# A triangular inverse carried through DRAM in fewer transfers, with longer steps behind it and behind a group norm

## The chip, the cores and the metric

The kernel runs on one core of one Trainium2 chip. The metric is the device time of one execution in microseconds (us). Two numbers are used: the time of a run, of which the median of three is given, and the span of one profiled execution, from its first instruction to its last. The engines are named as in the profile: PE (TensorE, matrix products), PEld (its weight loads), DVE (VectorE), ACT (ScalarE), POOL (GpSimd) and SP (SyncE, which here issues almost every DMA).

## What is computed

One inference step of a one-layer encoder over 16 meta tokens, 256 prompt tokens and 64 sample tokens, with a model width of 2048. One input projection feeds two branches: a Mamba-2 scan (SSD, 32 heads in 4 groups) and a gated DeltaNet (16 heads, in 4 groups of 4 here). Their outputs go through one output projection and are merged by sigmoid gates; an MLP with squared ReLU and a final norm follow. The two places that the change touches are these:

```python
# SSD branch, once for each group
ya = _rmsnorm(ya.reshape(b, l, SSD_GROUPS, -1), ssd_norm_w.reshape(SSD_GROUPS, -1))

# DeltaNet branch, once for each block of 64 tokens and each head
lmat = jnp.where(strict, bc[..., :, None] * jnp.einsum('bhtk,bhsk->bhts', kc, kc) * decay, 0.0)
tinv = lax.linalg.triangular_solve(eye + lmat, jnp.broadcast_to(eye, lmat.shape),
                                   left_side=True, lower=True, unit_diagonal=True)
u = jnp.einsum('bhts,bhsv->bhtv', tinv, vc * bc[..., None])
```

## The kernel before

All matrix products with weights are done in three passes on split operands: a weight tile `raw` comes by DMA (512 KB, a slice of 512 rows by 256 columns), ACT copies its rounded part to `hi` (line 61, a helper), DVE subtracts to get `lo` (line 64, a helper), and PE runs 24 matmuls on a slice (8 places times three passes; `hi` with the high and the low part of the activations, `lo` with the high part), writing `pbig`. `raw`, `hi` and `lo` have three buffers each. A block is 4 slices of an input or gate projection, or 1 slice of an output projection.

**Main work and side work.** `run(main, side)` interleaves two generators. `main` is weight matmuls and yields the nominal microseconds of each three passes; `side` is a scan (`scan_ssd` or `scan_gdn`), which emits some instructions and then yields a number: so many nominal microseconds of main work are put ahead of its next instructions. That number is no wait on the chip; it only places instructions. What is left of `side` when `main` has ended is emitted at once. PE keeps exactly this order (`manual_schedule` for PE); the order on the other engines and of the DMAs on SP comes from a scheduler which orders by readiness. Every engine then runs its own list in order and waits on semaphores.

The runs that matter here are, in this order: `scan_ssd(0)` beside `proj_ssd(1)`; `scan_ssd(1)` and `scan_ssd(2)` each beside an output projection and the next input projection; `scan_ssd(3)` beside `out_a(2)` and `proj_gdn(0)`; then `scan_gdn(0)` beside `out_a(3)`, `gate_a` and `proj_gdn(1)`; `scan_gdn(1)` and `scan_gdn(2)` beside an output projection and the next DeltaNet projection; `scan_gdn(3)` beside `out_b(2)` and `gate_b`. Then come the last output projection and the MLP, with next to no side work.

**The SSD norm.** In `scan_ssd`, for each of three chunks `c`: ACT squares `yz` into `sq`, POOL adds its four parts in two instructions, then `yield 7.0` (line 718). `rstd_bcast` (line 594) sums over the partitions with a matmul into `prs`, DVE scales it (`r`, line 599), POOL takes the power -0.5, DVE spreads it over a diagonal (`dg`, line 602), then `yield 4.2`, and a matmul broadcasts it into `prb`. Four DVE instructions apply it to `yz`, ACT rounds that to `yh` and DVE takes the rest `yl`. After chunk 2 of group 0 the output projection `out_a(0)` reads `yh` and `yl` directly behind the run.

**The triangular inverse.** In `scan_gdn`, each of 12 matrices (3 chunks, 4 heads) of 128x128 is inverted by diagonal blocks of 32x32 first. The matrices `a` are stored to the DRAM scratch `aD`; `diag(ad, c)` (line 135) views the 16 diagonal blocks of one chunk, one block to a partition, and they are loaded into `ab`, twice (partitions 0 to 47 and 64 to 111, since each half of the partitions solves 16 of the 32 columns). The substitution (line 844) runs 31 steps on DVE, `s` from 30 down to 0: a product `pr` and a reduction into column `s` of `ubt` (line 851), each step yielding 0.5 + 0.0028 times its size. Step `s` writes column `s` alone, and columns 16 to 31 are final once `s` = 15 is done. When all steps are done:

- ACT copies `ubt`, transposed, into `ub` (line 856, two instructions of 48x512), and three DMAs store `ub` to the diagonal blocks of `uD` (line 858);
- two DMAs store `ubt` to `uTD` (line 861);
- three DMAs load the whole matrices from `uD` into `u` (line 863, one for each chunk);
- three DMAs load transposed blocks from `uTD` into `tr` (line 869).

Then `yield 9.6` (line 871), and PE joins the blocks: first `pz` from `tr` and `a` (32x32), then `ptr` and `pu` with `u`, then the same for 64x64. The copy `z` of `pz`, the three chunks' outer loop and the state update follow.

Of the kernel before, what the change touches and what calls it, by code (L numbers as in the profile page):

```python
# [8 lines left out]
F32 = mybir.dt.float32  # L9
# [5 lines left out]
P = 128  # L15
# [11 lines left out]
BS = 32  # L27
# [15 lines left out]
def tile_hybrid_step(ctx: ExitStack, tc: tile.TileContext, i: dict, o: dict):  # L43
    nc = tc.nc
# [15 lines left out]
    def act(out, in_, func=AF.Copy, **kw):  # L60
        nc.scalar.activation(out=out, in_=in_, func=func, **kw)  # L61

    def tt(eng, out, a, b, op):
        eng.tensor_tensor(out=out, in0=a, in1=b, op=op)  # L64
# [67 lines left out]
    def whole(t, c, n=P):  # L132
        return t[c, :, :P * P].rearrange("h (s t) -> s h t", t=P)[:n, :, :n]

    def diag(t, c):
        r = t[c].rearrange("h (b r) -> (h b) r", r=BS * P + BS)
        return r[:, :BS * P].rearrange("q (s t) -> q s t", t=P)[:, :, :BS]


# [454 lines left out]
    def rstd_bcast(pool, ssum, n, width):  # L594

        pc = scr("prs")
        mm(pc[:n, 256:257], ssum[:, :n], ones[:, 0:1])
        r = pool.tile([P, 1], F32, tag="r1", name="r1", bufs=2)
        V.tensor_scalar(out=r[:n], in0=pc[:n, 256:257], scalar1=1.0 / width, scalar2=EPS, op0=MUL, op1=ADD)
        tt(G, r[:n], r[:n], nhalf_pow[:n, 0:1], ALU.pow)  # L600
        dg = pool.tile([P, P], F32, tag="dg", name="dg", bufs=2)
        V.tensor_scalar(out=dg[:n, :n], in0=ident[:n, :n], scalar1=r[:n, 0:1], scalar2=None, op0=MUL)
        yield 4.2
        pr = scr("prb")
        mm(pr[:, :n], ones[:n, :], dg[:n, :n])
        return pr[:, :n]

    def scan_ssd(g, sg, x4, bc, z4):
# [25 lines left out]
        for c in range(3):  # L634
            lo, n, l0, nl, o0 = CH_LO[c], CH_N[c], L_LO[c], L_N[c], O_LO[c]
# [79 lines left out]
            act(sq[:, :, :nl], yz[:, :, :nl], AF.Square)  # L715
            tt(G, sq[:, 0:2, :nl], sq[:, 0:2, :nl], sq[:, 2:4, :nl], ADD)
            tt(G, sq[:, 0, :nl], sq[:, 0, :nl], sq[:, 1, :nl], ADD)
            yield 7.0
            rb = yield from rstd_bcast(sg, sq[:, 0, :], nx, 512)
            rb = rb[:, :nl]  # L720
            yh, yl = ys[g] = ys.get(g) or new_y()
# [15 lines left out]
    def scan_gdn(g, sg, q4, k4, v4, z4):  # L737
        heads = range(4)
        hsl = slice(32 + g * 4, 32 + g * 4 + 4)
        ad, ud = aD[g % 2], uD[g % 2]  # L740
        def t2k(tag, name, bufs):
            return sg.tile([P, 4, P], F32, tag=tag, name=name, bufs=bufs)
# [25 lines left out]
        for c in range(3):  # L768
            lo, n, l0, nl, o0 = CH_LO[c], CH_N[c], L_LO[c], L_N[c], O_LO[c]
# [54 lines left out]
        NB = 12 * (P // BS)  # L824
        nb, HB = NB // 3, BS // 2
        NE = 64 + NB
        ab = sg.tile([P, BS, BS], F32, tag="TZ", name="ab", bufs=1)
        G.memset(ab, 0.0)

        ubt = t2k("Ak", "ubt", 1).rearrange("p h (t s) -> p (h t) s", s=BS)  # L830
        uf = ubt.rearrange("p t s -> p (t s)")
        G.memset(uf, 0.0)
        for e in range(2):
            b = slice(e * 64, (e + 1) * 64)
            for c in range(3):
                nc.sync.dma_start(ab[e * 64 + c * nb:e * 64 + (c + 1) * nb], diag(ad, c))
            o1 = e * HB
            G.memset(uf[b, o1:o1 + (HB - 1) * (BS + 1)].rearrange("p (s t) -> p s t", t=BS + 1)[:, :, 0], 1.0)
            o1 += (HB - 1) * (BS + 1)
            G.memset(uf[b, o1:o1 + 1], 1.0)  # L840

        af = ab.rearrange("p s t -> p (s t)")[:NE, :HB * (BS + 1)]
        yield 4.8
        G.memset(af.rearrange("p (s t) -> p s t", t=BS + 1)[:, :, 0], 1.0)
        for s in range(BS - 2, -1, -1):
            j0, r0 = (s + 1 - HB, s + 1) if s >= HB else (0, s)
            w, m = HB - j0, BS - r0
            pr = t2k("sq", "pr", 2).rearrange("p h c -> p (h c)")
            v = pr[:NE, :w * m].rearrange("p (t r) -> p t r", r=m)
            tt(V, v, ubt[:NE, j0:, r0:], ab[:NE, s:s + 1, r0:].to_broadcast([NE, w, m]), MUL)  # L850
            V.tensor_reduce(out=ubt[:NE, j0:, s], in_=v, axis=AX.X, op=ADD)  # L851
            yield 0.5 + 0.0028 * w * m
        u = sg.tile([P, 3, 4, P], F32, tag="U", name="u")
        ub = sg.tile([P, BS, BS], F32, tag="XW", name="ub", bufs=1)
        for e in range(2):
            act(ub[:NB, :, e * HB:(e + 1) * HB].rearrange("p s t -> p t s"), ubt[e * 64:e * 64 + NB])
        for c in range(3):
            nc.sync.dma_start(diag(ud, c), ub[c * nb:(c + 1) * nb])
        utd = uTD[g % 2]
        for e in range(2):  # L860
            nc.sync.dma_start(utd.rearrange("c h b t s -> (c h b) t s")[:, e * HB:(e + 1) * HB], ubt[e * 64:e * 64 + NB])
        for c in range(3):
            nc.sync.dma_start(u[:, c], whole(ud, c))

        tr = sg.tile([P, 12, 64], F32, tag="TZ", name="tr", bufs=1)
        G.memset(tr[:BS, :8, BS:], 0.0)
# [1 line left out]
            b0, b1 = b * BS, (b + 1) * BS  # L868
            nc.sync.dma_start(tr[b0:b1, :, (b % 2) * BS:(b % 2 + 1) * BS], utd[:, :, b].rearrange("c h t s -> t (c h) s"))
        tr = tr.rearrange("p (c h) t -> p c h t", h=4)  # L870
        yield 9.6

        for r, pairs, cs in ((32, (0, 64), (0, 1, 2)), (64, (0,), (0, 1))):
            every = [(q, c, h) for c in cs for h in heads for q in pairs if q == 0 or c]
# [4 lines left out]
            for q, c, h in every:  # L879
                b, d = slice(q, q + r), slice(q + r, q + 2 * r)  # L880
# [14 lines left out]
            for q, c, h in every:  # L895
                b, d = slice(q, q + r), slice(q + r, q + 2 * r)
                mm(pu[b, c, h], z[d, c, h], u[d, c, h, d])
            for q in pairs:
                b, d, c0 = slice(q, q + r), slice(q + r, q + 2 * r), 1 if q else 0
                V.tensor_copy(u[b, c0:len(cs), :, d], pu[b, c0:len(cs)])  # L900
            yield 1.5
        for c in range(3):
            lo, n, l0, nl, o0 = CH_LO[c], CH_N[c], L_LO[c], L_N[c], O_LO[c]
# [150 lines left out]
    with ExitStack() as sctx:  # L1054
        sg = sctx.enter_context(tc.tile_pool(name="sg", bufs=1))
        run(kept(proj_ssd(1), tiles), scan_ssd(0, sg, *tiles[0]))
        run(chain(out_a(0), kept(proj_ssd(2), tiles)), scan_ssd(1, sg, *tiles[1]))
        run(chain(out_a(1), kept(proj_ssd(3), tiles)), scan_ssd(2, sg, *tiles[2]))
        run(chain(out_a(2), kept(proj_gdn(0), tiles)), scan_ssd(3, sg, *tiles[3]))
    with ExitStack() as sctx:  # L1060
        sg = sctx.enter_context(tc.tile_pool(name="sgg", bufs=1))
        run(chain(out_a(3), gate_a(), kept(proj_gdn(1), tiles)), scan_gdn(0, sg, *tiles[4]))
        run(chain(out_b(0), kept(proj_gdn(2), tiles)), scan_gdn(1, sg, *tiles[5]))
        run(chain(out_b(1), kept(proj_gdn(3), tiles)), scan_gdn(2, sg, *tiles[6]))
        run(chain(out_b(2), gate_b()), scan_gdn(3, sg, *tiles[7]))

        hnh, hnl = new_u("hn")
        h2 = const.tile([P, NO], F32, name="h2")

        def normed(k):  # L1070
            d, w = acc[:, k, :], par[:, NP_ + k:NP_ + k + 1]
            act(hnh[:, k, :NO], d, AF.Copy, scale=w)
            stt(hnl[:, k, :NO], d, w, hnh[:, k, :NO].bitcast(F32), MUL, SUB)

        def merge(k, pt):
            d, q = acc[:, k, :], ftile("q")
            tt(V, q, sgb[k // 4][:, k % 4, :], pt, MUL)
            tt(V, d, d, q, ADD)
            if k >= LAG:
                normed(k - LAG)  # L1080

        run(out_proj(3584, ys[7], False, merge))
        for k in range(KD - LAG, KD):
            normed(k)
# [117 lines left out]
    with tc.manual_schedule():  # L1202
        for t in range(3):
            final_part(7, t)
            r, n = frs[:, t:t + 1], toks[t][1]
            stt(r[n], fss[n, t, 7:8], 1.0 / D, fsum[n, t:t + 1], MUL, ADD)
            tt(G, r[n], r[n], nhalf_pow[n, 0:1], ALU.pow)
        for m in range(2):
            for t, (_, n, t0) in enumerate(toks):
                dst = o["y_prompt"][0, t0:t0 + P, :] if t < 2 else o["y_sample"][0]  # L1210
                w, r = slice(m * H, (m + 1) * H), frs[n, t:t + 1]
# [36 lines left out]
```

## Time and profile before

| | before |
|---|---|
| median of 3 runs | 2376.53 us |
| lowest and highest of them | 2375.6 and 2377.53 us |
| the profiled execution, its time | 2375.45 us |
| its span | 2373.7 us |
| mean granted TensorE clock | 0.989 |
| DVE busy, share of the span | 1356.8 us, 57% |
| ACT busy | 1060.3 us, 45% |
| POOL busy | 345.9 us, 15% |
| moved by DMA | 362.87 MB, mean 153 GB/s |

How to read the lines that follow below. A line of the waits names an engine, a line of the code, what it wrote, and what it waited for, with the total, the number of times and the longest. A line of the timeline has the start, the duration, the engine (SPq is the DMA issue on SP), the line, the operation, out<-in, and in brackets the idle time in front of it and what ended it. A line of the chain has start, duration, engine and name. A line of the windows has a stretch, its length, the busy time and count of PE, PEld, DVE, ACT and POOL, the granted TensorE clock (1.00 is full), the DMA engines' busy share and GB/s. Lines 58, 61, 64 and 67 are helpers, so the names of the tiles tell which work it is.

### The profile page before, as it was taken

How to read it: one execution, taken by the hardware profiler on the slowest of the kernel's cores; microseconds unless marked ns; L12 is line 12 of the kernel's file. 1: busy time of each engine (PE TensorE's matmuls, PEld its weight loads, DVE VectorE, ACT ScalarE, POOL GpSimd, SP SyncE). 2: the span in 40 equal slices, each digit the busy share in tenths (PEclk: the TensorE clock that was granted, in tenths of full speed). 3: DMA queues.
4: the chain of work that ended last, by engine and by line, in shares of the span. 5: the costliest groups of instructions: out<-in, count | busy, mean ns of one | idle time of the engine just before them, and what ended most of it. 6: DMA issues, size and time to landing. Idle time of an engine off the chain costs nothing.

```text
span 2373.7 us, 40688 instructions
## 1 busy us (share of the span) xinstructions
PE 2308.9 (97%) x16393; PEld 2284.7 (96%) x16393; DVE 1356.8 (57%) x2147; ACT 1060.3 (45%) x1822; POOL 345.9 (15%) x488
## 2 busy tenths in 40 slices
PE   7999999999999999899899999999999999999997
PEld 6999999999999999899899999999999999999997
DVE  6675858575855557568557558444444444444444
ACT  5655546355345544454454335433343234334433
POOL 3152515051211113112212110000000000000000
PEclk9999999999999999999899999999999999999999
DMA  7846555545556555454455544544554444445543
GB/s 194 222 123 182 143 158 154 156 131 172 158 166 185 150 152 144 127 154 134 127 152 149 158 144 149 148 151 151 151 151 150 146 150 151 150 151 151 169 142 115
DMA packets 411558, 362.87 MB, mean 153 GB/s; under 512 B 48841, under 2 KB 408346, under 8 KB 410906
## 3 DMA queue, kind: packets, MB, share of 16 engines
q1 hardware_dynamic: 411258, 360.15, 51.8%
q8 instruction: 128, 2.10, 0.4%
q14 instruction: 60, 0.49, 0.1%
q10 hardware_dynamic: 112, 0.13, 0.0%
HBM read 340.57 MB, written 19.66 MB: 152 GB/s over the span
## 4 chain that ended last, share of the span: by engine, by line
PE 85%; DVE 9%; DMA 2%; issue 1%; ACT 1%; POOL 1%; SPq 0%; ACTq 0%; DVEq 0%; POOLq 0%
PE pbig L58 78%; DVE lo L64 3%; DVE ubt L851 2%; DVE pr L64 1%; DVE c L67 1%; PE po L58 1%; DMA raw<-in_w_in_dram 1%; DMA tr<-uTD 1%; POOL yz L64 1%; PE pS L58 0%; PE pw L58 0%; ACT hi L61 0%; PE pkk L58 0%; PE pqk L58 0%; DVE ul L67 0%
## 5 line engine op out<-in xcount | busy, mean ns | idle before, releaser
L64 DVE TENSOR_TENSOR lo<-raw,hi 128x1024 fp32r<-128x1024 f32 x591 | 739.1, 1251 | 692.5 <-ACT hi L61 689.1
L61 ACT ACTIVATE hi<-raw 128x1024 fp32r<-128x1024 f32 x592 | 626.2, 1058 | 915.0 <-PE pbig L58 859.0
L58 PE MATMUL pbig<-uh,hi 128*128 128x320 f32 (+2 forms) x2176 | 692.5, 318 | 4.2 <-ACT uh L61 4.2
L58 PE MATMUL pbig<-uh,lo 128*128 128x320 f32 (+2 forms) x2176 | 683.9, 314 | 6.3 <-DVE lo L64 6.3
L58 PE MATMUL pbig<-ul,hi 128*128 128x320 f32 (+2 forms) x2176 | 685.0, 315 | 3.9 <-DVE ul L67 3.9
L58 PEld LDWEIGHTS pbig<-uh,hi 128*128 128x128 f32 x2176 | 413.5, 190 | 10.0 <-ACT uh L61 4.7
L58 PEld LDWEIGHTS pbig<-uh,lo 128*128 128x128 f32 x2176 | 413.4, 190 | 7.9 <-DVE lo L64 7.9
L58 PEld LDWEIGHTS pbig<-ul,hi 128*128 128x128 f32 x2176 | 413.5, 190 | 6.0 <-DVE ul L67 5.8
L58 PE MATMUL pbig<-hh,hi 128*128 128x320 f32 x1024 | 318.4, 311 | 0.0
L58 PE MATMUL pbig<-hnl,hi 128*128 128x320 f32 x1024 | 317.5, 310 | 0.0
L58 PE MATMUL pbig<-hl,hi 128*128 128x320 f32 x1024 | 316.7, 309 | 0.0
L58 PE MATMUL pbig<-hh,lo 128*128 128x320 f32 x1024 | 316.6, 309 | 0.0
L58 PE MATMUL pbig<-hnh,lo 128*128 128x320 f32 x1024 | 316.2, 309 | 0.0
L58 PE MATMUL pbig<-hnh,hi 128*128 128x320 f32 x1024 | 315.5, 308 | 0.0
L58 PEld LDWEIGHTS pbig<-hnh,lo 128*128 128x128 f32 x1024 | 193.2, 189 | 0.0
L58 PEld LDWEIGHTS pbig<-hl,hi 128*128 128x128 f32 x1024 | 193.0, 188 | 0.0
L58 PEld LDWEIGHTS pbig<-hh,hi 128*128 128x128 f32 x1024 | 193.0, 188 | 0.0
L58 PEld LDWEIGHTS pbig<-hh,lo 128*128 128x128 f32 x1024 | 192.9, 188 | 0.0
L58 PEld LDWEIGHTS pbig<-hnh,hi 128*128 128x128 f32 x1024 | 192.7, 188 | 0.2
L58 PEld LDWEIGHTS pbig<-hnl,hi 128*128 128x128 f32 x1024 | 192.4, 188 | 0.0
L58 PE MATMUL pbig<-yh,hi 128*128 128x320 f32 x512 | 161.4, 315 | 0.0
L58 PE MATMUL pbig<-yl,hi 128*128 128x320 f32 x512 | 157.7, 308 | 0.3 <-DVE yl L64 0.3
(303 smaller groups left out, 2436.8 us busy)
## 6 DMA issues: line engine op xcount, KB each, us to landing
raw<-in_w_in_dram SPq DMA_DIRECT2D x256, 512.0 KB, 3.8
raw<-in_w_up_dram SPq DMA_DIRECT2D x128, 512.0 KB, 3.8
raw<-in_w_down_dram SPq DMA_DIRECT2D x128, 512.0 KB, 3.4
raw<-in_w_out_dram SPq DMA_DIRECT2D x64, 512.0 KB, 3.5
raw<-in_w_in_dram SPq DMA_DIRECT2D x32, 256.0 KB, 3.5
em<-rowd SPq DMA_DIRECT2D x8, 512.0 KB, 7.7
u<-uD SPq DMA_DIRECT2D x12, 256.0 KB, 3.8
eab<-rowd SPq DMA_DIRECT2D x8, 336.0 KB, 8.5
```

The source lines that it names most:

```text
L58: nc.tensor.matmul(out, lhsT=lhsT, rhs=rhs, start=start, stop=stop, **kw)
L61: nc.scalar.activation(out=out, in_=in_, func=func, **kw)
L64: eng.tensor_tensor(out=out, in0=a, in1=b, op=op)
L67: nc.vector.scalar_tensor_tensor(out=out, in0=a, scalar=s, in1=b, op0=op0, op1=op1)
L851: V.tensor_reduce(out=ubt[:NE, j0:, s], in_=v, axis=AX.X, op=ADD)
```

## The change

Four edits; nothing else of the program text differs.

1. `diag` views all three chunks at once. So `ab` is loaded by two DMAs in place of six, `ub` is stored by one in place of three, and `u` is loaded by one in place of three. The bytes and the pieces that they consist of are the same.
2. `ub` is allocated ahead of the substitution, and its copy is cut by columns: columns 16 to 31 are copied (two ACT instructions of 48x16x16) at the head of step `s` = 14, the other half when the substitution is done.
3. The step behind the DMAs yields 15.0 in place of 9.6.
4. The step behind the sum of squares in `scan_ssd` yields 8.4 in place of 7.0.

```diff
-    def diag(t, c):
-        r = t[c].rearrange("h (b r) -> (h b) r", r=BS * P + BS)
+    def diag(t):
+        r = t.rearrange("c h (b r) -> (c h b) r", r=BS * P + BS)
...
-            yield 7.0
+            yield 8.4
             rb = yield from rstd_bcast(sg, sq[:, 0, :], nx, 512)
...
-            for c in range(3):
-                nc.sync.dma_start(ab[e * 64 + c * nb:e * 64 + (c + 1) * nb], diag(ad, c))
+            nc.sync.dma_start(ab[e * 64:e * 64 + NB], diag(ad))
...
+        def rows(s0):
+            for e in range(2):
+                act(ub[:NB, s0:s0 + HB, e * HB:(e + 1) * HB].rearrange("p s t -> p t s"), ubt[e * 64:e * 64 + NB, :, s0:s0 + HB])
+
         for s in range(BS - 2, -1, -1):
+            if s == HB - 2:
+                rows(HB)
...
-        for e in range(2):
-            act(ub[:NB, :, e * HB:(e + 1) * HB].rearrange("p s t -> p t s"), ubt[e * 64:e * 64 + NB])
-        for c in range(3):
-            nc.sync.dma_start(diag(ud, c), ub[c * nb:(c + 1) * nb])
+        rows(0)
+        nc.sync.dma_start(diag(ud), ub[:NB])
...
-        for c in range(3):
-            nc.sync.dma_start(u[:, c], whole(ud, c))
+        nc.sync.dma_start(u.rearrange("p c h t -> p (c h) t"), ud.rearrange("c h r -> (c h) r")[:, :P * P].rearrange("n (s t) -> s n t", t=P))
...
-        yield 9.6
+        yield 15.0
```

On PE the order changes only in place. Counted in the two programs, the first `pz` of DeltaNet groups 0, 1, 2 and 3 stands 39, 42, 42 and 39 weight matmuls later. In SSD group 0 the `prs` of chunk 1 stands 21 weight matmuls later, chunk 2's first `pyo` 21 later, chunk 2's `prs` 30 later and its `prb` 24 later, which is the end of that run's weight matmuls: `out_a(0)` follows directly, where 24 weight matmuls stood between before. In groups 1 to 3 the `prs` of the last chunk stands 30 to 33 later and 87 or more weight matmuls still follow `prb` in the run.

On SP, behind the substitution of DeltaNet group 1, the DMAs stood before as follows (`uTD`, `uD` the scratch in DRAM, `raw` a weight slice):

```order
L861 DMA uTD_112<-ubt 48x512 x2
L858 DMA uD_110<-ub 16x32x32 x3
L863 DMA u<-uD_110 128x4x128 x2
L869 DMA tr<-uTD_112 32x12x32
L863 DMA u<-uD_110 128x4x128
L869 DMA tr<-uTD_112 32x12x32 x2
L198 DMA raw<-in_w_in_dram 128x4x256 x5
```

In the changed program the same place reads:

```order
L865 DMA uTD_112<-ubt 48x512
L862 DMA uD_110<-ub 48x32x32
L865 DMA uTD_112<-ubt 48x512
L198 DMA raw<-in_w_in_dram 128x4x256
L866 DMA u<-uD_110 128x12x128
L872 DMA tr<-uTD_112 32x12x32 x3
L198 DMA raw<-in_w_in_dram 128x4x256 x7
```

All `tr` loads now stand behind the single `u` load, which waits for the whole store of `ub`, and one weight slice stands between. In groups 0 and 3 two `tr` loads stand ahead of `u` and one behind it.

On DVE, at the end of the first SSD run (`r`, `dg` and `yz` belong to chunk 2 of group 0; `em` is the decay tile of group 1's first chunk, which comes by DMA), the difference of the two programs is:

```order
-L599 TENSOR_SCALAR r_2119<-prs 128x1
-L602 TENSOR_SCALAR dg<-ident,r_2119 128x128
-L664 TENSOR_SCALAR em<-em,acs 128x128 x4
-L64 TENSOR_TENSOR lo<-raw,hi 128x1024
-L664 TENSOR_SCALAR em<-em,acs 128x128 x4
+L664 TENSOR_SCALAR em<-em,acs 128x128 x8
+L599 TENSOR_SCALAR r_2155<-prs 128x1
+L602 TENSOR_SCALAR dg<-ident,r_2155 128x128
+L64 TENSOR_TENSOR lo<-raw,hi 128x1024
 L67 SCALAR_TENSOR_TENSOR yz<-yz,par,prb 128x128 x4
 L64 TENSOR_TENSOR yl<-yz,yh 128x4x128
```

The eight instructions on `em` move from behind `dg` to ahead of `r`, so `r` and `dg`, and with them `prb`, come after the transfer that brings `em`.

On ACT, in DeltaNet group 0, the two rows `ub<-ubt 48x16x32 x2` stood together behind the substitution. Now two pairs of half the size stand there, one of them within it (`sgt` is the sigmoid of the gate):

```order
+L61 ACTIVATE ub<-ubt 48x16x16 x2
+L61 ACTIVATE hi<-raw 128x1024
+L61 ACT_TABLE_LOAD
+L61 ACTIVATE sgt<-pbig 128x320
+L61 ACTIVATE hi<-raw 128x1024
+L61 ACTIVATE sgt<-pbig 128x320
+L61 ACTIVATE hi<-raw 128x1024 x3
+L61 ACTIVATE sgt<-pbig 128x320
+L61 ACTIVATE hi<-raw 128x1024
+L61 ACTIVATE sgt<-pbig 128x320
+L61 ACTIVATE hi<-raw 128x1024 x2
+L61 ACTIVATE ub<-ubt 48x16x16 x2
```

The first pair moved ahead of the second by eight weight splits and four `sgt`. On DVE no instruction of the substitution waits for ACT in either program.

More of the change, by code (lines that the diff above doesn't have):

```diff
@@ L844, in scan_gdn @@
         G.memset(af.rearrange("p (s t) -> p s t", t=BS + 1)[:, :, 0], 1.0)
+        ub = sg.tile([P, BS, BS], F32, tag="XW", name="ub", bufs=1)
+        def rows(s0):
+            for e in range(2):
+                act(ub[:NB, s0:s0 + HB, e * HB:(e + 1) * HB].rearrange("p s t -> p t s"), ubt[e * 64:e * 64 + NB, :, s0:s0 + HB])
         for s in range(BS - 2, -1, -1):
+            if s == HB - 2:
+                rows(HB)
             j0, r0 = (s + 1 - HB, s + 1) if s >= HB else (0, s)
@@ L853, in scan_gdn @@
         u = sg.tile([P, 3, 4, P], F32, tag="U", name="u")
-        ub = sg.tile([P, BS, BS], F32, tag="XW", name="ub", bufs=1)
-        for e in range(2):
-            act(ub[:NB, :, e * HB:(e + 1) * HB].rearrange("p s t -> p t s"), ubt[e * 64:e * 64 + NB])
-        for c in range(3):
-            nc.sync.dma_start(diag(ud, c), ub[c * nb:(c + 1) * nb])
+        rows(0)
+        nc.sync.dma_start(diag(ud), ub[:NB])
         utd = uTD[g % 2]
```

## The prediction

> **What bounds the kernel now.** I read the page first, then PE's waits, then for each stretch in which PE waits the timelines, the chain and the windows.
>
> ```profile
> PE 2308.9 (97%) x16393; PEld 2284.7 (96%) x16393; DVE 1356.8 (57%) x2147; ACT 1060.3 (45%) x1822; POOL 345.9 (15%) x488
> PE pz L58 <- DMA tr<-uTD: 24.3, 8, 7.4
> PE prs L58 <- POOL sq L64: 3.7, 4, 1.6
> ```
>
> PE is busy for 97% of the span and its order is fixed, so the kernel is the sum of its matmuls and of what PE waits. The change adds no matmul and removes none; it can only change waits, and the speed at which PE works around them. The two waits that it aims at are the first and one of the next in the list: 24.3 us and 3.7 us. They are met four times each, once for each group (eight entries for `pz`, since it waits for two of the three `tr` loads).
>
> ```profile
> PE pz L58 <- DMA tr<-uTD: 4.5, 2, 3.4
> PE pz L58 <- DMA tr<-uTD: 8.1, 2, 7.4
> PE pz L58 <- DMA tr<-uTD: 7.6, 2, 7.1
> PE pz L58 <- DMA tr<-uTD: 4.0, 2, 3.3
> ```
>
> These are the same wait in groups 0, 1, 2 and 3 of the DeltaNet scan, each from the waits of a window around it.
>
> ```profile
> 674.30:677.70 3.40, 3.40 (x39) 3.34 (x40) 0.00 (x0) 0.86 (x2) 1.08 (x2) 0.50 0.95 290
> 969.90:974.60 4.70, 4.69 (x45) 4.29 (x46) 0.00 (x0) 0.86 (x2) 0.26 (x1) 0.50 0.49 163
> 1153.40:1162.40 9.00, 9.00 (x107) 8.54 (x108) 0.97 (x2) 1.23 (x3) 0.26 (x1) 0.50 0.26 86
> 1335.10:1339.90 4.80, 4.78 (x48) 4.39 (x49) 0.17 (x1) 1.92 (x3) 0.00 (x0) 0.50 1.07 352
> 970.97 3.54 PE pbig L58 x12
> 1036.04 27.64 PE pbig L58 x189
> ```
>
> The windows behind the four waits show a second cost that the list of waits hides. PE is busy all through them, but at a granted clock of 0.50: 3.4 + 4.7 + 9.0 + 4.8 = 21.9 us. The chain says what that means: there 12 weight matmuls took 3.54 us (0.295 each), where 189 undisturbed ones took 27.64 (0.146 each). So the work in these 21.9 us would take about 11.0 us less at full clock. The waits cost not 24.3 but some 35 us.
>
> **The DeltaNet part.** How long must the step be? Group 0, from the last reduction of the substitution to the arrival of `tr`:
>
> ```profile
> 662.47 0.69 DVE L851 TENSOR_REDUCE ubt<-pr 112x16 f32<-112x512 f32 x1
> 663.19 2.35 ACT L61 ACTIVATE ub<-ubt 48x512 f32<-48x512 f32 x2 [2.26 <-DVE ubt L851]
> 665.57 1.46 SPq L858 DMA_DIRECT2D uD<-ub  x3
> 667.87 0.93 SPq L863 DMA_DIRECT2D u<-uD  x2
> 670.45 3.71 DMA tr<-uTD
> 674.21 1.01 PE pz L58 x30
> 665.50:668.30 2.80, 2.80 (x21) 2.80 (x20) 1.64 (x3) 2.77 (x5) 0.00 (x0) 1.00 0.50 66
> ```
>
> The reduction ends at 663.16 and `pz` runs at 674.21: 11.0 us. PE stood ready 4.5 us earlier, at 669.7, which is 6.5 us after the reduction. The change puts 39 (groups 0, 3) or 42 (groups 1, 2) weight matmuls in between, at 0.146 us 5.7 or 6.1 us. So if the chain stays as long as it is, group 0 has 6.5 + 5.7 = 12.2 us for 11.0, and group 3, whose wait was 4.0, the like.
>
> Does the chain stay as long? The copy into `ub` on it halves: 1.2 us in place of 2.35. Of the three stores one is issued, 0.5 us in place of 1.46, but `u` must wait for all of it. The first of the three was there 2.3 us after its issue (665.57 to 667.87). A store three times as large is not in the trace. From below it lands as that one did, in 2.3; from above three follow each other, 6.9. The window of these stores decides which is nearer: the DMA engines were half busy for 2.8 us with all three in it, 1.4 us of work at most, so two thirds more of it, 0.9 us, comes on top of 2.3, and I take 3.2. Then one issue of `u` (0.47, half of the 0.93 for two), three of `tr` at the same rate, and 3.7 until the last lands, as now: 1.2 + 0.5 + 3.2 + 0.5 + 1.4 + 3.7 = 10.5 us. The fewer transfers thus give only 0.5 us; it is the longer step that takes the wait away.
>
> ```profile
> 956.91 0.68 DVE L851 TENSOR_REDUCE ubt<-pr 112x16 f32<-112x512 f32 x1
> 969.91 1.06 PE pz L58 x30
> 1141.64 0.69 DVE L851 TENSOR_REDUCE ubt<-pr 112x16 f32<-112x512 f32 x1
> 1153.38 1.05 PE pz L58 x30
> ```
>
> In groups 1 and 2 less time is left. The reductions end at 957.6 and 1142.3, `pz` runs at 969.9 and 1153.4, and without its wait it would have stood at 961.8 and 1145.8, 4.2 and 3.5 us after the reduction. With 6.1 more that is 10.3 and 9.6 us for a chain of 10.5, plus 0.5 for the issue of the weight slice that the new order puts ahead of `u`. So 0.7 and 1.4 us of wait are left. Against that, the new order has the last reduction two weight splits earlier on DVE in these groups, which may take it away; I keep 1.0 for both together. The term is **-23.3 us** (from -24.3 to -10).
>
> The clock follows the wait. A wait of 1.5 us left it at 1.00 (the row of 164.00 below), one of 3.4 us and more did not. With no wait over 1.5 us the 11.0 us go. The small matmuls of 32x32 in these windows may not scale with the clock; were it the weight matmuls alone, the loss by the chain's rows of this kind is near 8 us. I take the middle, **-9.5 us** (from -11 to -3). [...]
>
> The early copy into `ub` stands on ACT, which is busy for 45% of the span; its 1.2 us are hidden by that idle time. If the cover were gone, a weight split would come 1.2 us later, four times. The merged loads of `ab` start behind the last store of `a`, where three of the six stood before; the substitution hides them.
>
> **The SSD part.** In groups 1 to 3 the longer step removes the wait of `prs`: 3.7 less the 1.5 of group 0 is **-2.2 us**, and the 1.4 nominal us cost nothing, since 87 and more weight matmuls still follow. Group 0 is different:
>
> ```profile
> PE prs L58 <- POOL sq L64: 1.5, 1, 1.5
> 164.00:165.00 1.00, 0.07 (x1) 0.07 (x1) 0.00 (x0) 0.99 (x2) 0.80 (x2) 1.00 0.00 0
> 192.59 0.29 DVE L602 TENSOR_SCALAR dg<-ident,r 128x128 f32<-128x128 f32 x1 [0.67 <-POOL r L64]
> 196.26 0.88 DVE L664 TENSOR_SCALAR em<-em,acs 128x128 f32<-128x128 f32 x4 [3.38 <-DMA em<-rowd]
> 198.97 1.12 DVE L67 SCALAR_TENSOR_TENSOR yz<-yz,par,prb 128x128 f32<-128x128 f32 x4
> 200.79 0.69 DVE L64 TENSOR_TENSOR yl<-yz,yh 128x512 fp32r<-128x512 f32 x1 [0.70 <-ACT yh L61]
> 201.53 0.41 PE L58 MATMUL pbig<-yl,hi 128*128 128x320 f32 x1 [0.31 <-DVE yl L64]
> ```
>
> Now `out_a(0)` needs `yl` at 201.53 and waits 0.3 us for it. In the new order nothing stands between `prb` and `out_a(0)`, and DVE does the eight `em` before `r` and `dg`. `em` comes by a transfer that SP issues behind `eab`, and `eab` overwrites what `yo` reads, which follows `pyo`: 21 weight matmuls later, 3.1 us, less the 1.5 us that PE no longer waits for chunk 1, so 1.6. The transfer therefore ends between 196.3, as now, and 197.9; I take 197. From there: `em` 2 x 0.88, then `r`, the power on POOL and `dg` 1.2 (0.2 for `r`, the 0.7 us wait, 0.3), `prb` 0.4, a weight split 1.2, `yz` 1.1, 0.7 until `yh` is there, `yl` 0.7, in all 7.1: 204.1 in place of 201.5. That is **+2.6 us**, the saved 1.5 in chunk 1 being in it already (from -1.8, if `em` comes early and nothing waits, to +3.5).
>
> **Sum.** -23.3 - 9.5 - 2.2 + 2.6 = -32.4. From the profiled execution's 2375.45 that is 2343.05; the median of the runs lies 1.08 above that execution, so **2344.1 us**.
>
> **The rivals.** *Weight loads held up on SP.* While SP waits for the store to land, no weight slice is issued, and PE no longer stands still meanwhile.
>
> ```profile
> 672.03 1.72 SPq L198 DMA_DIRECT2D raw<-in_w_in_dram  x3
> raw<-in_w_in_dram SPq DMA_DIRECT2D x256, 512.0 KB, 3.8
> L64 DVE TENSOR_TENSOR lo<-raw,hi 128x1024 fp32r<-128x1024 f32 x591 | 739.1, 1251 | 692.5 <-ACT hi L61 689.1
> L61 ACT ACTIVATE hi<-raw 128x1024 fp32r<-128x1024 f32 x592 | 626.2, 1058 | 915.0 <-PE pbig L58 859.0
> ```
>
> In group 0 the next slice was issued at 672.03, 8.9 us after the reduction; 3.8 to land, 1.1 and 1.3 to split, so ready 15.1 us after it. PE, at `pz` 15 matmuls into a slice, has 57 more until the slice that it is for, three on: 669.7 + 8.3 = 678.0, or 14.9 us after the reduction, were it not for the wait. With the chain 0.5 us shorter this just meets. If the store lands late, or in groups 1 and 2, where SP's queue is fuller, each group gives 1 to 3 us back, with 1 to 2 us of clock: 8 to 16 us less gain, **2352 to 2360**. For it: the margin is a few tenths. Against: the scheduler has put one slice more ahead of `u` in groups 1 and 2.
>
> *The clock falls at the end of the first SSD run.* PE stands there for 2 to 3 us at `prb` and, behind eight transposes, for 2 us at `yh` and `yl`. If these count as one pause, the half rate of group 0 to 3 follows, 3.4 to 4.8 us of work at half: 1.7 to 2.4 us, **2346**. By the rows 1.5 us of pause do nothing and 3.4 us do; this lies between. [...]
>
> *One large transfer is slower than three: slower than before.* The pieces are 128 bytes for `uD`; if the store takes 6.9 us, and the load of `u`, as one, three times the 3.7 us of the `tr` row above, 11.1, where its three loads overlap now, `tr` behind it lands 1.2 + 0.5 + 6.9 + 0.5 + 11.1 + 3.7 = 23.9 us after the reduction. PE would be at `pz` at 12.2 (or 9.6 to 10.3), so it would wait 12 to 14 us in each group against 4 to 8 now: 52 in place of 24, with the clock's loss unchanged, **2404**. It decides from the point at which the chain grows by more than the step gives, 5.7 to 6.1 us. Against it: 1.4 us of engine time for all pieces of the store.
>
> *The wait moves with the step: no change.* If the substitution ended later by as much as `pz`, nothing would be gained, **2377**. Its instructions wait for nothing on PE but the weight splits between them, and in the new order these are no more than before, and fewer in groups 1 and 2. This is also the case that the early copy does not do what it says: if DVE had to wait for ACT's reading of `ubt`, the chain would lengthen by ACT's queue. The order shows no such wait.
>
> **How the numbers follow.** The forecast 0.64; the clock at the first run's end 0.16; weight loads held up 0.13; no change 0.04; slower 0.03. The likeliest gives 2344.1. All lower ends of the terms, -24.3 - 11 - 2.2 - 1.8 = -39.3, give 2337 (with the 1.08). The upper end takes in most of the held-up weights, 2358. Beyond lie the last two cases and some of the third, 0.1 to 0.15. A measurement of this kernel can tell 0.2%, 4.8 us, from no change: faster by more than that are the first three, 0.93; within it 0.04; slower 0.03.
>
> **What would show it.** Right: `pz` waits for `tr` under 3 us in all, the granted clock stays at 1.00 behind all four `pz`, `prs` is gone from PE's waits, and a new entry of 2 to 5 us stands there for `prb` on `dg` and `pbig` on `yh` or `yl` near 200 us. The term of the store is right if the `uD` store lands within 3.5 us. Wrong: a wait of `pbig` on `hi` or `lo` of several us within 10 us behind each `pz` (weights held up), `u` or `tr` landing more than 16 us after the last reduction (large transfers slower), or a clock of 0.50 behind `pz` in spite of short waits.

## The result, and the profile after

The changed kernel takes 2341.97 us (median of four runs, 2339.8 to 2343.7) against 2376.95 for the kernel before, run beside it: a ratio of 0.985 (95% interval 0.9834 to 0.9865). The profiled execution took 2343.37 us with a span of 2341.5, so the span is 32.2 us shorter; the prediction's sum was 32.4.

From the page of the changed kernel, its engine line; then the four longest entries of its list of PE's waits (total, times, longest), without those of the start of the kernel:

```profile
PE 2300.9 (98%) x16393; PEld 2278.7 (97%) x16393; DVE 1354.5 (58%) x2147; ACT 1065.4 (46%) x1830; POOL 333.1 (14%) x488
PE ph L58 <- DVE xwr L64: 6.1, 4, 1.9
PE pz L58 <- DMA tr<-uTD: 1.2, 1, 1.2
PE pbig L58 <- ACT yh L61: 1.1, 1, 1.1
PE pbig L58 <- DVE lo L64: 0.7, 1, 0.7
```

And two lines of the kernel before's list that the prediction left out:

```profile
PE pbig L58 <- DVE lo L64: 6.3, 5, 1.6
PE ph L58 <- DVE xwr L64: 0.2, 1, 0.2
```

The `tr` wait went from 24.3 to 1.2, as forecast, and `prs` left the list. But a wait of 6.1 us stands at the top that the prediction did not have (`ph`, the state update of the SSD scan, for DVE's `xwr`), and the 6.3 us for `lo`, which it did not speak of, have gone too.

The windows of the changed kernel, for the stretches around the only two losses of clock behind its start while PE had work (stretch, length, PE busy, clock, DMA share, GB/s):

```profile
394.20:397.50 3.30, 1.38 (x10) 1.00 0.14 48
397.60:401.00 3.40, 3.40 (x15) 0.50 0.28 72
1134.90:1138.20 3.30, 2.21 (x47) 1.00 1.08 314
1138.30:1145.10 6.80, 6.80 (x77) 0.50 0.49 142
```

One is behind a `ph` wait, one behind the 1.2 us of `pz` that are left in group 2. Added up over windows of 1 us behind the start (busy time times what the clock lacks of 1.00), the kernel before lost 12.0 us of matmul time and the changed one 5.1. That counts every matmul as twice as long at 0.50, as the weight matmuls were (0.295 us against 0.146), which is too much for the 32x32 ones: 30 of `pz` took 1.01 us at 674.21 in the kernel before, nearly all at 0.50 (34 ns each), and 40 took 1.15 us at 1135.99 in the changed one, at 1.00 (29 ns each). So the 6.9 us between the two sums are an upper bound.

| term | predicted, us | measured, us |
|---|---|---|
| `tr` waits | -23.3 | -23.1 |
| half clock | -9.5 | -6.9 at most (12.0 to 5.1) |
| `prs` waits, SSD groups 1 to 3 | -2.2 | -2.2 |
| SSD group 0: `prs` (-1.5), `yh` (+1.1) | +2.6 | -0.4 |
| `ph` waits for `xwr` | none | +5.9 |
| `lo` waits | none | -5.6 |
| `ptr`, `pcum`, `po` | none | +1.1 |
| sum | -32.4 | -31.2 of 32.2 |

What remains, 1.0 us and whatever the clock's row has too much, is in none of these rows and was not taken apart. The total is right, but not every row of the sum, so the experiments take the change apart.

### The profile page after: what moved, and what is told of

Same layout as the page of the kernel before. It is cut to its first block, busy times and chain, and to the rows that moved or that the text cites. A ratio compares the mean times of both kernels' runs of the same rounds, so it can differ in the third digit from the quotient of the medians.

```text
span 2341.5 us, 40643 instructions
## 1 busy us (share of the span) xinstructions
PE 2300.9 (98%) x16393; PEld 2278.7 (97%) x16393; DVE 1354.5 (58%) x2147; ACT 1065.4 (46%) x1830; POOL 333.1 (14%) x488
## 4 chain that ended last, share of the span: by engine, by line
PE 90%; DVE 5%; DMA 2%; ACT 1%; issue 1%; SPq 1%; POOL 0%; ACTq 0%; DVEq 0%
PE pbig L58 84%; DVE lo L64 1%; DMA raw<-in_w_in_dram 1%; PE po L58 1%; DVE pr L64 1%; DVE ubt L858 1%; PE pS L58 0%; DVE c L67 0%; PE pyd L58 0%; PE pw L58 0%; PE pkk L58 0%; PE pqk L58 0%; ACT hi L61 0%; PE ph L58 0%; DMA x<-in_x_sample_dram 0%
```

## Which edit carries the gain

The theory behind the prediction: the longer step takes the `tr` wait and the half clock away, the fewer transfers give 0.5 us per group, the norm's step nearly nothing. The rivals: the transfers carry the gain; or the norm's step is a loss, since its order brings the `ph` waits. The kernel before ran beside every group of runs, at 2377.9 to 2379.1 us.

**The step alone.** The kernel before with `yield 9.6` made `yield 15.0`.

> The kernel before with one number changed: the step behind the inverse's DMAs yields 15.0 in place of 9.6; the transfers, the copy and the norm's step stay as before. Theory A, the longer step is what takes the tr wait away: PE reaches pz 12.2, 10.3, 9.6 and about 12 us after the last reduction, for a chain that stays at 11.0, so the wait falls from 24.3 to 2 to 4 us, the half clock behind most of the four pz goes, and the time falls by 24 to 31 us, to 2346 to 2353. Theory B, the fewer transfers and the early copy are what shortens the chain: more than 2 us of tr wait are left in each group, the clock stays at 0.50 behind them, and the time falls by less than 18 us, to over 2359.

Measured: 2349.95 us (2349.4 to 2353.2), ratio 0.988 (0.9865 to 0.9895); the `tr` wait is 2.7 us. The step alone gives 28 of the 35 us.

**The merges and the early copy alone.** The changed kernel with `yield 15.0` back at 9.6 and `yield 8.4` at 7.0.

> The changed kernel with both steps put back (9.6 behind the DMAs, 7.0 in the norm), so that only the fewer transfers and the early half copy are left of the change. Theory A: the chain shortens by 0.5 us in each group, 2 us in all, the clock stays at 0.50 behind the four pz, and the time is 2373 to 2377. Theory B, the transfers carry the gain: the tr wait falls below 14 us and the time below 2362. A third way, a large transfer lands so much later that the tr wait grows above 24.3 us: over 2378.

Measured: 2367.43 us (2364.6 to 2370.7), ratio 0.9954 (0.9941 to 0.9966), between the two theories. The `tr` wait is 20.5 us, near the 22 of theory A, but the `lo` waits are at 0.7: the merges give 10 us and not 2.

**The norm's step alone, and the change without it.** The kernel before with `yield 8.4`; the changed kernel with `yield 7.0`.

> The kernel before with only the norm's step at 8.4 in place of 7.0. The prediction's theory: prs waits of 3.7 us go and the end of the first run costs 2.6 net, so the time stays within 2 us of before, 2375 to 2379. The theory formed from the profile after: the norm's yl and the next chunk's xwr now stand on DVE behind cb and xt and run beside POOL's em product, ph waits some 6 us for xwr and the first run's end 1 us for yh, so the time is 2 to 6 us above before, 2379 to 2383, with ph in the list of waits at 5 to 7 us.

> The changed kernel with only the norm's step put back to 7.0. If the norm's step was worth what the prediction said (2.2 gained in groups 1 to 3, 2.6 lost in group 0), this runs as the changed kernel does, 2340 to 2344. If it is a loss by the ph waits: prs waits of about 3.7 us come back, ph (6.1) and yh (1.1) go, with 1.6 us of half clock behind one ph, and the time is 2336 to 2339.

Measured: 2382.78 (2380.7 to 2384.4), ratio 1.002 (1.0011 to 1.0029), with 6.1 us of `ph` waits; and 2336.90 (2336.7 to 2338.8), ratio 0.9827 (0.9814 to 0.9841). Both say that the norm's step costs 5 us, and without it the changed kernel is faster than with it. The prediction had it at +0.4.

## Why `ph` waits

In SSD group 0, chunk 2, the timelines of the kernel before and of the changed one (start, duration, engine, line, operation). Before:

```profile
173.81 0.68 DVE L64 TENSOR_TENSOR yl<-yz,yh 128x512 fp32r<-128x512 f32 x1
174.41 0.29 DVE L64 TENSOR_TENSOR cb<-pcb,trib 128x128 f32<-128x128 f32 x1
174.61 1.13 DVE L64 TENSOR_TENSOR xwr<-xw,xwr 128x512 fp32r<-128x512 f32 x1
175.15 3.96 POOL L64 TENSOR_TENSOR em<-em,cb 128x512 f32<-128x512 f32 x2
```

After:

```profile
175.37 0.28 DVE L64 TENSOR_TENSOR cb<-pcb,trib 128x128 f32<-128x128 f32 x1
175.57 0.68 DVE L64 TENSOR_TENSOR xt<-pxt,dt 128x512 f32<-128x512 f32 x1
175.74 2.97 POOL L64 TENSOR_TENSOR em<-em,cb 128x512 f32<-128x512 f32 x2 [2.06 <-DVE cb L64]
176.17 1.41 DVE L64 TENSOR_TENSOR yl<-yz,yh 128x512 fp32r<-128x512 f32 x1
177.50 1.75 DVE L64 TENSOR_TENSOR xwr<-xw,xwr 128x512 fp32r<-128x512 f32 x1
179.31 0.73 PE L58 MATMUL ph<-xwr,bt 64*128 64x512 f32 x4 [1.59 <-DVE xwr L64]
```

The later norm makes DVE do `cb` ahead of `yl` and `xwr`. As soon as `cb` is there, POOL starts its two products of `em`, and both DVE instructions take 1.41 and 1.75 us beside them. The order alone, or POOL beside it? The experiment puts the two products on DVE, where they fall in behind `xwr`, and leaves the order ahead of them as it is:

```diff
-                tt(G, em[:n, a:a + 4, :nl], em[:n, a:a + 4, :nl], cb[:n, None, :nl].to_broadcast([n, 4, nl]), MUL)
+                tt(V, em[:n, a:a + 4, :nl], em[:n, a:a + 4, :nl], cb[:n, None, :nl].to_broadcast([n, 4, nl]), MUL)
```

> The changed kernel (norm's step 8.4) with the two products of em and cb in the SSD scan computed on DVE in place of POOL; on DVE they stand behind xwr, and nothing in front of xwr moves. Theory A, DVE's yl (1.41 us) and xwr (1.75) are slow because POOL works on em beside them: yl takes 0.68 and xwr about 1.1, ph waits less than 2 us in all in place of 6.1, and the time falls by 3 to 6 us, to 2336 to 2339. Theory B, it is the new order on DVE alone that makes xwr late: yl and xwr take as long as in the changed kernel, ph waits 5 us and more, and the time is 2341 to 2345.

The same place in that run, by its timeline:

```profile
175.81 0.69 DVE L64 TENSOR_TENSOR yl<-yz,yh 128x512 fp32r<-128x512 f32 x1
176.42 0.68 DVE L64 TENSOR_TENSOR xwr<-xw,xwr 128x512 fp32r<-128x512 f32 x1
177.02 1.71 DVE L64 TENSOR_TENSOR em<-em,cb 128x512 f32<-128x512 f32 x2
177.75 0.96 PE L58 MATMUL ph<-xwr,bt 64*128 64x512 f32 x6
```

`yl` takes 0.69, `xwr` 0.68, no `ph` wait is left, and the time is 2333.41 us (2332.7 to 2336.8), ratio 0.9815 (0.98 to 0.983): 8.6 us less than the changed kernel, more than theory A expected. `cb` and `xt` still stand ahead of `yl` and `xwr` there, so it is POOL's work beside them that makes the two late, and not the order alone. `yl` took 0.69 us without POOL's `em` beside it and 1.41 with it, `xwr` 0.68 and 1.75. What of the chip the two engines share there is not shown.

## What the merges do

**Only `ab` merged, and only `u` merged.** Both with `yield 15.0` and `yield 7.0`; the first on the kernel before, the second on the changed one with this edit (`diag_of` views one chunk, as `diag` did before):

```diff
-            nc.sync.dma_start(ab[e * 64:e * 64 + NB], diag(ad))
+            for c in range(3):
+                nc.sync.dma_start(ab[e * 64 + c * nb:e * 64 + (c + 1) * nb], diag_of(ad, c))
```

> The kernel before with the step at 15.0 and the six ab loads merged into two; the stores and loads of u, its copy and the norm's step stay as before. Measured against the run with the step alone (2349.95) and the one with all but the norm's step (2336.9). Theory A, the merged ab loads put DVE's first substitution steps into another place among the weight splits and so take away the waits of pbig for lo: lo falls from 7.3 us to about 0.7, pz stays at 2 to 4 us, and the time is 2338 to 2344. Theory B, the 13 us come from the one store and load of u and the early copy: lo stays above 6 us and the time is 2347 to 2352.

> The changed kernel with the norm's step at 7.0 and ab loaded by six DMAs again, so that of the merges only those of u and the early copy are left. Theory A (the ab loads carry the lo waits): lo is at 6 to 7.5 us, the tr wait at 1 to 2 us, and the time is 2344 to 2350. Theory B (u carries it): lo about 0.7, 2336 to 2340.

Measured: 2342.34 us (2339.1 to 2345.6), ratio 0.985 (0.9834 to 0.9867); and 2363.74 (2359.7 to 2369.8), ratio 0.9942 (0.9924 to 0.9959). From PE's waits of the two, first `ab` merged, then `u` merged:

```profile
PE pbig L58 <- DVE lo L64: 1.4, 3, 0.7
PE pbig L58 <- ACT hi L61: 1.4, 1, 1.4
```

```profile
PE pz L58 <- DMA tr<-uTD: 10.8, 4, 3.8
PE pbig L58 <- DVE lo L64: 6.6, 5, 1.6
```

The `ab` loads carry the `lo` waits, as theory A had it. How: in the kernel before the first substitution steps stand on DVE ahead of a weight split, with `acc` instructions between them that wait for PE (group 2, timelines of ACT, DVE and PE):

```profile
1095.12 1.06 ACT L61 ACTIVATE hi<-raw 128x1024 fp32r<-128x1024 f32 x1 [2.46 <-PE pbig L58]
1097.03 0.49 DVE L64 TENSOR_TENSOR acc<-acc,pbig 128x320 f32<-128x320 f32 x1 [0.81 <-PE pbig L58]
1099.39 1.22 DVE L64 TENSOR_TENSOR lo<-raw,hi 128x1024 fp32r<-128x1024 f32 x1
1100.66 0.42 PE L58 MATMUL pbig<-uh,lo 128*128 128x336 f32 x1 [1.60 <-DVE lo L64]
```

`hi` was ready at 1096.2 and `lo` began at 1099.4. With two `ab` loads the first product comes behind that split. The substitution also ends earlier against PE. The last reduction and the first `pz` of group 2, with the step alone and then with `ab` merged:

```profile
1133.54 0.69 DVE L851 TENSOR_REDUCE ubt<-pr 112x16 f32<-112x512 f32 x1
1143.23 0.50 PE L58 MATMUL pz<-tr,a 32*32 32x32 f32 x10
```

```profile
1126.03 0.68 DVE L854 TENSOR_REDUCE ubt<-pr 112x16 f32<-112x512 f32 x1
1138.05 1.33 PE L58 MATMUL pz<-tr,a 32*32 32x32 f32 x40
```

PE stands at `pz` 9.0 us after the reduction in the one and 11.3 in the other. The prediction had the merge of `ab` at nothing ("the substitution hides them").

The merge of `u` (with the early copy), without that of `ab`, makes the kernel slower than the step alone by 14 us, which neither theory expected: `tr` comes later, not earlier. In all four groups of that run `pz` waits and starts 12.6 to 13.1 us after the reduction. In the changed kernel, group 2 (timeline of DVE and SP; the last line is from the chain):

```profile
1122.73 0.68 DVE L858 TENSOR_REDUCE ubt<-pr 112x16 f32<-112x512 f32 x1
1124.87 0.33 SPq L862 DMA_DIRECT2D uD<-ub  x1
1128.59 0.38 SPq L866 DMA_DIRECT2D u<-uD  x1
1129.45 3.02 SPq L872 DMA_DIRECT2D tr<-uTD  x3
1135.99 1.15 PE pz L58 x40
```

The store lands in 3.7 us (1124.87 to 1128.59; the prediction took 3.2). But from the issue of `u` to `tr` in place it is 7.4 us, where the prediction took 0.5 + 1.4 + 3.7 = 5.6. Nearly all of the difference is in the issues: the three of `tr` take 3.02 us on SP, not 1.4, while the last lands 3.5 us behind them. Why an issue takes longer there is not shown. So the chain is 12.6 us, where the prediction had 10.5 and 0.5 for the weight slice.

**`u` in three, with the early copy; and the whole copy late.** Both from the changed kernel with `yield 7.0`: the store and load of `u` as loops over the three chunks again; or

```diff
-            if s == HB - 2:
-                rows(HB)
...
-        rows(0)
+        for e in range(2):
+            act(ub[:NB, :, e * HB:(e + 1) * HB].rearrange("p s t -> p t s"), ubt[e * 64:e * 64 + NB])
```

> The changed kernel with the norm's step at 7.0 and u stored and loaded by three DMAs each again; the merged ab loads and the early half copy stay. Measured against the run with all but the norm's step (2336.9; its only tr wait is 1.74 us in group 2, 13.1 us behind the reduction). Theory A, the one store and one load of u make the chain longer and not shorter: with three, pz finds tr 10.5 to 11.5 us after the last reduction and waits nowhere; the time is 2333 to 2338, or up to 2343 if a weight split is held up behind the additional DMAs on SP, as a wait of pbig for hi then shows. Theory B (the prediction's, 0.5 us shorter with one): the tr wait grows to 2 to 4 us and the time to 2339 and more, without a wait for hi.

> The changed kernel with the norm's step at 7.0 and the whole copy into ub behind the substitution again, as two instructions. Theory A, the early half takes 1 us off the chain: the store of uD is issued 2.4 us after the last reduction in place of 1.45, the tr wait rises from 1.7 us to 3 to 5 (groups 1 and 2, some in 0), with half clock behind one or two of them, and the time is 2339 to 2346. Theory B, the store is not what tr waits for: 2335 to 2338.

Measured: 2342.66 us (2338.1 to 2344.6), ratio 0.9843 (0.9828 to 0.9857), with no `tr` wait at all and a `hi` wait of 1.4 us in group 1; and 2338.37 (2337.5 to 2341.9), ratio 0.9826 (0.981 to 0.9843), with 3.0 us of `tr` waits. So one transfer does lengthen the chain (1.7 us of `tr` wait in group 2 with one, none with three), and its use is on SP: with one, a weight slice is issued ahead of `u` (3.2 us after the reduction in group 1), with three only behind `tr` (7.8 us), and PE then waits for `hi`. This is the rival of the held-up weight loads, at 1.4 to 2 us in one group. The half clock behind that wait costs more. In the run with `u` in three (stretch, length, PE busy, clock, DMA share, GB/s):

```profile
966.80:976.90 10.10, 10.10 (x85) 0.50 0.50 154
```

That is up to 5 us, counted as above. The run with only `ab` merged has the same `hi` wait and 13.6 us at 0.50 behind it. The run with all but the norm's step has neither, and is 5 to 6 us faster than both. The early copy brings the store forward by 1 us (from 2.4 to 1.45 us after the reduction); its 1.5 us in the time are within the spread of the runs and stay open.

## Repairs

**A still longer step.** The changed kernel with `yield 7.0` and `yield 17.0`; then the kernel with `em` on DVE and `yield 17.0`.

> The changed kernel with the norm's step at 7.0 and the step behind the DMAs at 17.0 in place of 15.0. Theory A: the one wait for tr that is left (1.7 us in group 2) goes and nothing else comes, 2334 to 2337. Theory B: what follows pz is pressed against the end of its run and waits on the copies between the joins, 2338 or more.

> The changed kernel with the products of em and cb on DVE and the step behind the DMAs at 17.0. If the two repairs add up (the ph waits stay away, the tr wait of 1.9 us and its half clock of 3.4 us lost go), the time is 2328 to 2332, the lowest of all; if the longer step gives as much back elsewhere, 2333 and more.

Measured: 2335.32 us (2334.8 to 2335.6), ratio 0.982 (0.9805 to 0.9835), no `tr` wait; and 2332.81 (2332.1 to 2334.4), ratio 0.9805 (0.979 to 0.982), neither a `tr` wait nor a window at half clock behind the start. The second lies between its two expectations.

**`tr` ahead of `u`.** With `em` on DVE and the step at 15.0, the stores of `uTD` and the loads of `tr` are written ahead of the copy into `ub`:

```diff
-        rows(0)
-        nc.sync.dma_start(diag(ud), ub[:NB])
         utd = uTD[g % 2]
         for e in range(2):
             nc.sync.dma_start(utd.rearrange("c h b t s -> (c h b) t s")[:, e * HB:(e + 1) * HB], ubt[e * 64:e * 64 + NB])
-        nc.sync.dma_start(u.rearrange("p c h t -> p (c h) t"), ud.rearrange("c h r -> (c h) r")[:, :P * P].rearrange("n (s t) -> s n t", t=P))
...
             nc.sync.dma_start(tr[b0:b1, :, (b % 2) * BS:(b % 2 + 1) * BS], utd[:, :, b].rearrange("c h t s -> t (c h) s"))
+        rows(0)
+        nc.sync.dma_start(diag(ud), ub[:NB])
+        nc.sync.dma_start(u.rearrange("p c h t -> p (c h) t"), ud.rearrange("c h r -> (c h) r")[:, :P * P].rearrange("n (s t) -> s n t", t=P))
```

> The changed kernel with the products of em and cb on DVE, and with the stores of uTD and the three loads of tr written ahead of the copy into ub, so that on SP the tr loads stand in front of the load of u in all four groups; the step stays at 15.0. Measured against the run with em on DVE alone (2333.4; tr waits of 1.9 us with 6.8 us at half clock behind them in group 2). Theory A, tr is late in groups 1 and 2 because it stands behind the 768 KB of u: issued ahead of it, tr is there 8 to 11 us after the last reduction, pz waits nowhere, u still arrives in time for ptr, and the time is 2328 to 2333. Theory B, tr is late for another reason (its own store, or the weight slices on the DMA engines): pz still waits 1 us and more in groups 1 and 2, and the time stays at 2333 to 2337.

Measured: 2332.18 us (2331.7 to 2334.2), ratio 0.9807 (0.9794 to 0.9821), without a `tr` wait. The DMA issues (count, KB each, median us from issue to landing) of the kernel before, the changed kernel and this one:

```profile
tr<-uTD SPq DMA_DIRECT2D x12, 48.0 KB, 3.7
```

```profile
u<-uD SPq DMA_DIRECT2D x4, 768.0 KB, 5.5
tr<-uTD SPq DMA_DIRECT2D x12, 48.0 KB, 5.1
```

```profile
u<-uD SPq DMA_DIRECT2D x4, 768.0 KB, 6.3
tr<-uTD SPq DMA_DIRECT2D x12, 48.0 KB, 1.9
```

And the issues of `tr` in group 2 of this run:

```profile
1120.25 1.34 SPq L869 DMA_DIRECT2D tr<-uTD  x3
```

The same 48 KB land in 5.1 us in the changed kernel, where eight of the twelve loads stand behind the 768 KB of `u`, and in 1.9 where all stand ahead of them. The three issues take 1.34 us and not 3.02. By these numbers `tr` is there some 7 us after the reduction (1115.97), where the changed kernel needed 12.6. Whether a step shorter than 15.0 then does as well was not tried. With `em` on DVE, this and the 17.0 are two ways to the same time, 9 to 10 us below the changed kernel.

## Why the prediction came out right, point by point

- **The bound and the two waits: right.** PE's list of waits was the kernel's account, and the longer step is what removes the `tr` wait: it alone gives 28 us.
- **The `tr` term: right in sum, from two errors that cancel, which is luck.** In group 2 the prediction had 10.5 us of chain, 0.5 of a weight slice's issue and PE at `pz` after 9.6, so 1.4 of wait; measured are 12.6, with that issue in it, and 11.4, so 1.2. The chain was 1.6 us too short: the three issues of `tr` behind the one load of `u` take 3.0 us and not 1.4. (The store, at 3.7 us, also lies above the 3.5 that the prediction gave as its sign.) PE's arrival was 1.8 us too early because the `ab` merge was priced at nothing; the prediction saw the last reduction move ahead of two weight splits, but allowed only 1.1 us for it in groups 1 and 2 together. Without that merge the chain's growth would have cost 8 us more of `tr` wait (10.8 against 2.7 us).
- **The clock term: half right.** Behind three of the four `pz` the half clock is gone. But its rule, that a wait of up to 1.5 us leaves the clock at 1.00, failed: in group 2 a wait of 1.2 us was followed by 6.8 us at 0.50, which is one of the prediction's own signs of being wrong. The term is -6.9 at most, for -9.5. A longer wait, 1.58 us, cost nothing in one run and a window at 0.50 in another (last section).
- **The SSD term: wrong.** The step of the prediction that failed is "the 1.4 nominal us cost nothing, since 87 and more weight matmuls still follow". It looked at PE's order and at group 0's end alone. The price was paid on DVE at the head of the next chunk, in all groups, 5.9 us of `ph` waits, and more with the clock. The end of group 0 came out better than forecast (`pbig` on `yl` at 203.14, for 204.1): `em` was there at 195.85 and not at 197, `prb` did not wait, and `yh` cost 1.1. The rival of a falling clock there did not come.
- **The `lo` term was missing**: 5.6 us, in the list of waits and not asked about, since the change did not seem to touch weight splits.

That the sum came out is luck as well. The `ph` waits (5.9 us), the clock (at least 2.6) and the small new waits (1.1) made the forecast too good; the `lo` waits (5.6), the end of group 0 (3.0) and the rest that was not taken apart (at least 1.0) made it too bad by as much.

## What to carry to other kernels

When a step is moved, read the new order of every engine at the place that it moves to, not only at the place that it leaves, and ask which engine starts work beside it: here `yl` took 1.41 us beside POOL in place of 0.69. Merging transfers changed three things here: what was queued behind landed later (`tr` in 5.1 us from its issue, 3.7 before), other loads got earlier issue slots (a weight slice 3.2 us after the reduction in place of 7.8), and the work that waited for the transfers got a new order (the `lo` waits fell from 6.3 to 0.7 us). Each can be a gain or a loss. What the longer step left of the long wait (1.9 us with `em` on DVE) was fed by a small load, and it ended when that load was issued ahead of the large one: the 48 KB of `tr` then landed in 1.9 us.

## What the runs showed of the hardware

In these runs the half clock came in whole windows, on a grid that stayed fixed within a run. In windows of 0.1 us, the stretches at 0.50 behind the start (without the last 10 us of the span, in which PE has no work) last 3.4, 10.2, 13.6 and 6.8 us in the kernel before, 3.4 and 6.8 in the changed one: one to four times 3.41. The prediction measured only the parts in which PE was busy throughout (9.0 of 13.6, for example). Within one run all these falls lie on one grid of 3.413 us. In windows of 0.02 us, the clock of the kernel before falls at 674.30, 964.43, 1148.75 and 1333.07, that is 290.13, 184.32 and 184.32 us apart, or 85, 54 and 54 times 3.413; that of the changed one at 397.59 and 1138.29, 740.69 us apart, or 217 times. So here it depended on where the grid lay in a run whether a pause fell into one window or was cut by two. The same `prs` wait of 1.58 us near 494, in the kernel before and in the run with the step alone:

```profile
493.82 0.38 PE L58 MATMUL prs<-ones,sq 128*128 128x1 f32 x2 [1.58 <-POOL sq L64]
490.00:493.30 3.30, 2.23 (x15) 1.00 0.57 159
493.40:496.80 3.40, 2.98 (x20) 1.00 0.23 35
```

```profile
494.19 0.38 PE L58 MATMUL prs<-ones,sq 128*128 128x1 f32 x2 [1.58 <-POOL sq L64]
491.20:494.50 3.30, 1.72 (x13) 1.00 0.42 143
494.60:498.00 3.40, 3.40 (x13) 0.50 0.47 119
```

In the first an edge of the grid (493.4, which is 53 windows ahead of the fall at 674.3) cuts the wait and nothing follows; in the second the wait lies in one window, and the next runs at 0.50. The grid lies elsewhere in the second run than in the first (an edge at 494.6 there), so for this pause the price was chance. PE was not idle in all windows ahead of a fall: it was busy for 1.72 of 3.30 us ahead of this fall, and for 1.38 ahead of that at 397.6, while 2.23 of 3.30 had no consequence. Ahead of the fall at 1138.3 it was busy for 2.21, of which 1.15 were the 32x32 matmuls of `pz`; whether these count for less was not tried. How little work in a window brings the fall is not shown beyond these four.
